# Attention-output units: last two operands made before the next unit's first, two operands to one ring tile

## Chip, cores, metric

One core of one Trainium2 chip. The metric is the device time of one execution in microseconds (us), lower being better. Three runs of the kernel before took 2354.53, 2354.87 and 2357.86 us, with a median of 2354.87 us.

## What is computed

One layer of a streaming encoder step, for 512 new frames of one stream and 64 frames of a second, cached one; the kernel carries all 576 frames side by side as columns. The reference, cut to what matters here:

```python
proj = rmsnorm(x, g_norm1) @ w_in            # 2048 -> 6144
o_attn = stick_breaking_blocks(q, k_all, v_all, P)   # 8 heads x 128
o_conv = gb * conv                            # 1024 channels
mix = concatenate([rmsnorm(o_attn, g_attn_out), rmsnorm(o_conv, g_conv_out)])
x = x + mix @ w_out                           # 2048 x 2048
x = x + (silu(h2 @ w_gate) * (h2 @ w_up)) @ w_down
```

The change sits in the product of the normed attention output with the upper half of `w_out` (rows 0 to 1023), which comes after the convolution's units and before the product with the lower half.

## The kernel before, in words

**Stages.** The heads' projections and the attention come first, then the convolution's columns of `w_in`, then the attention's half of `w_out`, then the convolution's half (`out_proj`, line 1256), then the feed-forward units. Every product is in fp32 made of two fp32r parts: a weight is split into a high part (a copy on ACT) and a low part (a subtraction on DVE), frames likewise, and three matmuls give one product.

**Attention-output units.** From line 993 on, the list `CU` holds nine convolution units and then eight output units, which this text calls U0 to U7 (in the code n = 9 to 16, kind `"o"`, `NCU` being 9). A unit is a block of 256 output columns against 1024 rows of `w_out`. It is done by a seven-product scheme for 2 by 2 blocks: p1 to p7, each with its own weight operand, made of the four blocks a11, a12, a21, a22 of the weights and sums of them. Here U3 p4 means product 4 of unit U3. One product of an output unit is 12 matmuls of 128 x 288 on 4 slices of 128 x 128 weights.

**Loads.** `call_columns` (line 1001) loads a unit's raw weights, 1 MB, with one DMA on SP's queue (line 1014) into one of the two places of `raw_a`. A place is called for again when the last operand that reads it (p3 and p4 of the unit that holds it) has been prepared (lines 1063 to 1067). So a unit's load goes out once p3 and p4 of the unit two before it are done.

**Making operands.** `conv_prepare` (line 1026) makes one operand. Before p6 it makes the sums own = a21 + a22 (line 1043), a21 -= a11 (line 1044) and a11 = own - a11 (line 1046), before p3 a12 -= a11 (line 1050), all on DVE and mostly in place. Then comes the high part on ACT (line 1055) and the low part on DVE (line 1058). The operand lies in a tile `whl` of a ring of four: two tags, `whi` and `wlo`, with two buffers each, taken in turn (line 1053). A tile has room for 8 slices, and an output unit's operand fills 4 of them. A tile comes free when the product that reads it has run.

**Running products.** `conv_run` (line 1090) issues a product's matmuls and the evacuations. p1, p6 and p5 accumulate in one PSUM bank (`psy`), followed by p3; after each of the first three ACT copies the bank to a tile `part` (line 1095), and the next product on that bank waits for the copy. p7 and p4 share another bank (`psw`). DVE adds bank and part into the result `x2` (line 1106) after p2, after p5 (this one reads the `psw` bank, and p4 waits for it) and after p4 (this one frees the part that the next unit's p6 writes). ACT copies the last block after p3 (line 1104).

**Order.** `corder` (line 1209) is the order in which products run. From U3 on it reads, for unit n: n p1, then p3 and p4 of unit n-1, then n p2, p6, p7, p5 (the last unit, U7, goes on with p6, p7, p5, p2, p4, p3). After the product at place k the operand at place k+4 is prepared (line 1233). The program writes out the order of PE by itself, and SP's in this stage as well; on ACT and DVE the scheduler sets the order by its own estimate of when things are ready, and in the trace each of these engines keeps to the order that was built: an instruction that waits there holds up those behind it.

**Neighbours on the DMA engines.** SP also issues `mixm`, the convolution's normed output (line 1179, 2304 KB right behind U4's load, and another part right behind U7's). POOL issues, after each unit, an accumulating read of the residual input into `x2` (line 1182, 576 KB). After the stage come the split weights of `out_proj` (lines 177 and 178), which use the same ring.

## Time and profile before

| | us |
|---|---|
| median of three runs | 2354.87 |
| the profiled execution's own time | 2357.63 |
| span of its profile | 2355.9 |
| PE busy in the span | 2335.7 |
| stage of the output units, from the first matmul of U0 to the last of U7 | 682 to 774 |
| time of one product of an output unit, from one start to the next | 1.59 |

The profile is of one execution; times within it are counted from the start of the span, and 1.7 us lie outside the span. A row of the timeline shows start, duration, engine, line, operation, the tiles (out<-in) with their shapes, how many instructions were merged, and in brackets the idle time before with what ended it. The granted TensorE clock is 1.00 in every stage that matters here.

### The profile page before, as it was taken

To read this page: it belongs to the slowest core of one execution; us is meant where nothing else is said; L and a number is where in the kernel's file an instruction comes from. 1 tells how busy PE (TensorE), PEld (TensorE's weight loads), DVE (VectorE), ACT (ScalarE), POOL (GpSimd) and SP (SyncE) were. 2 spreads that over 40 slices of the span, in tenths; PEclk is the share of its full clock that TensorE was granted. 3 is DMA by queue.
4 is the path that set the end of the run, shared out by engine and by line. 5 is a ranking of instruction groups with operands and counts; after the bars stand their busy time and mean duration, and the time that the engine had idled before them with its cause. 6 is when DMAs were issued, how large, how long until landed. Compare 5 with 4: busy or idle time off the path is not lost.

```text
span 2355.9 us, 43774 instructions
## 1 busy us (share of the span) xinstructions
PE 2335.7 (99%) x17573; PEld 2326.5 (99%) x17573; DVE 1890.2 (80%) x2822; ACT 1138.5 (48%) x1989; POOL 298.6 (13%) x401
## 2 busy tenths in 40 slices
PE   9999999999999999999999999999999999999999
PEld 8999999989999999999999999999999999999999
DVE  7766665788887899888888888888888778887896
ACT  6655565434444555444444444444444444444444
POOL 1111111422121230000000000000000002431221
PEclk9999999999999999999999999999999999999999
DMA  8665563773468555344344444444444936885553
GB/s 267 164 167 145 135 163 108 247 232 114 124 235 225 177 170 162 123 154 152 123 153 137 139 153 140 135 153 128 148 153 131 355 122 201 226 238 189 199 133 101
DMA packets 581795, 395.74 MB, mean 168 GB/s; under 512 B 90718, under 2 KB 570712, under 8 KB 581592
## 3 DMA queue, kind: packets, MB, share of 16 engines
q1 hardware_dynamic: 572168, 376.28, 51.2%
q0 software_dynamic: 8624, 16.22, 3.3%
q8 instruction: 137, 2.24, 0.4%
q14 instruction: 66, 0.54, 0.1%
q10 hardware_dynamic: 800, 0.46, 0.1%
HBM read 301.46 MB, written 91.44 MB: 167 GB/s over the span
## 4 chain that ended last, share of the span: by engine, by line
PE 86%; DVE 8%; DMA 3%; ACT 2%; issue 1%; POOL 0%; SPq 0%; DVEq 0%; ACTq 0%; POOLq 0%
PE psy L1582 34%; PE psw L1582 17%; PE pj L221 13%; PE psx L1582 9%; PE psy L1086 5%; PE psw L1086 3%; PE psx L1086 1%; DMA raw_a<-in_w_out_dram 1%; DVE wlo L178 1%; DMA raw_a<-in_w_in_dram 1%; DVE whl L231 1%; DVE whl L1058 1%; PE z L723 1%; PE pjo L221 1%; PE po L794 1%
## 5 line engine op out<-in xcount | busy, mean ns | idle before, releaser
L1582 PE MATMUL psy<-h_s,whl 128*128 128x288 f32 x2787 | 411.1, 294 | 0.0
L221 PE MATMUL pj<-x,whi 128*128 128x288 f32 x1856 | 388.6, 298 | 0.3 <-DVE x L375 0.3
L1582 PEld LDWEIGHTS psy<-h_s,whl 128*128 128x128 f32 x2787 | 383.2, 188 | 0.1
L231 DVE TENSOR_TENSOR whl<-raw_a,whl 128x1024 fp32r<-128x1024 f32 (+4 forms) x296 | 322.4, 1090 | 56.7 <-ACT whl L230 55.4
L1582 PE MATMUL psw<-t,whl 128*128 128x288 f32 x2400 | 347.2, 294 | 0.0
L1582 PEld LDWEIGHTS psw<-t,whl 128*128 128x128 f32 x2400 | 327.8, 188 | 0.0
L230 ACT CAST whl<-raw_a 128x1024 fp32r<-128x1024 f32 (+4 forms) x296 | 267.9, 906 | 113.3 <-issue 35.6
L221 PEld LDWEIGHTS pj<-x,whi 128*128 128x128 f32 x1856 | 303.9, 189 | 1.1 <-DVE x L375 0.7
L221 PE MATMUL pj<-x,wlo 128*128 128x288 f32 x928 | 274.5, 296 | 0.1
L231 DVE TENSOR_TENSOR whl<-raw_b,whl 128x1024 fp32r<-128x1024 f32 (+5 forms) x190 | 198.1, 1042 | 65.9 <-ACT whl L230 65.0
L230 ACT CAST whl<-raw_b 128x1024 fp32r<-128x1024 f32 (+5 forms) x190 | 165.0, 871 | 169.8 <-issue 72.8
L1592 ACT COPY part<-psy 128x288 f32<-128x288 f32 x242 | 96.5, 399 | 273.9 <-PE psy L1582 271.2
L1582 PE MATMUL psy<-b22m,whl 128*128 128x288 f32 x1212 | 182.7, 294 | 0.8 <-ACT part L1592 0.8
L1582 PE MATMUL psy<-t2t,whl 128*128 128x288 f32 x1212 | 183.0, 294 | 0.0
L221 PEld LDWEIGHTS pj<-x,wlo 128*128 128x128 f32 x928 | 174.8, 188 | 0.7 <-DVE wlo L442 0.3
L1582 PE MATMUL psx<-h_s,whl 128*128 128x288 f32 x1185 | 173.5, 294 | 0.0
L1582 PEld LDWEIGHTS psy<-b22m,whl 128*128 128x128 f32 x1212 | 168.0, 188 | 1.0 <-ACT part L1592 1.0
L1582 PEld LDWEIGHTS psy<-t2t,whl 128*128 128x128 f32 x1212 | 168.3, 188 | 0.2 <-DVE whl L231 0.2
L1582 PEld LDWEIGHTS psx<-h_s,whl 128*128 128x128 f32 x1185 | 162.6, 188 | 0.0
L1361 POOL DMA_DIRECT2D hid_dram<-form x3 | 2.2, 749 | 947.2 <-DVE form L231 947.2
L230 ACT CAST whl<-s 128x1024 fp32r<-128x1024 f32 (+5 forms) x81 | 72.2, 892 | 99.4 <-PE psw L1582 99.2
L1582 PE MATMUL psy<-t,whl 128*128 128x288 f32 x576 | 106.6, 295 | 0.0
(474 smaller groups left out, 4306.6 us busy)
## 6 DMA issues: line engine op xcount, KB each, us to landing
hid_dram<-form SPq DMA_DIRECT2D x147, 288.0 KB, 2.3
raw_a<-in_w_in_dram SPq DMA_DIRECT2D x41, 1024.0 KB, 6.0
raw_a<-in_w_gate_dram SPq DMA_DIRECT2D x22, 1024.0 KB, 5.5
raw_a<-in_w_up_dram SPq DMA_DIRECT2D x22, 1024.0 KB, 5.9
raw_b<-in_w_gate_dram SPq DMA_DIRECT2D x22, 1024.0 KB, 6.6
raw_b<-in_w_up_dram SPq DMA_DIRECT2D x22, 1024.0 KB, 6.9
h_s<-hid_dram SPq DMA_DIRECT2D x10, 2016.0 KB, 12.3
raw_a<-in_w_out_dram SPq DMA_DIRECT2D x16, 1024.0 KB, 5.7
```

The source lines that it names most:

```text
L178: lo_eng.tensor_tensor(out=lo[:, a:b], in0=raw[:, a:b], in1=hi[:, a:b].bitcast(F32), op=ALU.subtract)
L221: mm(ps, w_[:, k, csl], x_, start=(k == 0 and n == 0), stop=(k == nk - 1 and n == 2))
L230: nc.scalar.copy(out=hi, in_=src)
L231: (lo_eng or nc.vector).tensor_tensor(out=lo, in0=src, in1=hi.bitcast(F32), op=ALU.subtract)
L723: mm(zb[i], a_[:, kk], b_[:, q0:TP], start=(n == 0), stop=False, skip_group_check=True)
L794: mm(po[:, i * P : 512], a_[:, i, :], b_[:, : 512 - i * P], stop=(i == 0 and n == 2), **kw)
L1058: tt(out=whl[:, 1], in0=src, in1=whl[:, 0].bitcast(F32), op=ALU.subtract)
L1086: mm(ps, whl[:, w_, j, :], x_, start=(start and j == 0 and q == 0), stop=(j == m - 1 and q == 2), skip_group_check=True)
L1361: q.dma_start(out=hid_dram[fp][2 * n - 2 : 2 * n].rearrange("f p t -> p f t"), in_=t.bitcast(F32))
L1582: mm(ps, whl[:, w_, j, :], x_, start=(start and j == 0 and q == 0), stop=(j == len(xs_) - 1 and q == 2), skip_group_check=True)
L1592: nc.scalar.copy(out=t, in_=st["y"])
```

## The change

Two things are done, both for output units alone.

Two operands share a tile of the ring. The first operand takes a tile and leaves its second half in `bt["pair"]`; the next takes that half and no tile of its own. The ring of four tiles then holds eight operands, and a tile comes free once both of its products have run.

The order of preparing is no longer the order of running. From U3 on, in `porder`, p3 and p4 of unit n-1 are prepared ahead of n p1. The products run as before.

```diff
         src = at[p_]
         cturn[0] += 1
-        whl = wpool.tile([P, 2, NP, P], F32R, tag=("whi", "wlo")[cturn[0] % 2], name="whl")[:, :, :m]
+        if early or "pair" not in bt:
+            whl = wpool.tile([P, 2, NP, P], F32R, tag=("whi", "wlo")[cturn[0] % 2], name="whl")
+            if not early:
+                bt["pair"] = whl[:, :, m:]
+            whl = whl[:, :, :m]
+        else:
+            cturn[0] -= 1
+            whl = bt.pop("pair")
         coper[n, p_] = whl
...
+    porder = list(corder)
+    for k_, (n, p_) in enumerate(corder):
+        if p_ == 1 and n > NCU + 2:
+            porder[k_ : k_ + 3] = [*corder[k_ + 1 : k_ + 3], (n, p_)]
...
         for q in begin[k_] if k_ < len(begin) else range(k_ + 4, min(k_ + 5, len(corder))):
-            conv_prepare(*corder[q])
+            conv_prepare(*porder[q])
```

Built, the changed kernel has the same instructions in the same order on PE, SP and POOL. On ACT and DVE the order differs inside this stage alone.

## Prediction

> **What bounds the kernel now.** I read the page first: its span, the row of the engines and the chain's shares.

> ```profile
> span 2355.9 us, 43774 instructions
> PE 2335.7 (99%) x17573; PEld 2326.5 (99%) x17573; DVE 1890.2 (80%) x2822; ACT 1138.5 (48%) x1989; POOL 298.6 (13%) x401
> PE 86%; DVE 8%; DMA 3%; ACT 2%; issue 1%; POOL 0%; SPq 0%; DVEq 0%; ACTq 0%; POOLq 0%
> ```

> PE is busy all but 20 us of the span. The change keeps its matmuls and their order, so a gain can only come out of PE's idle time, and only inside the stage of the output units. The view of busy time by stretches, the waits of PE around this stage, and its timeline give that:

> ```profile
> 682.00:774.00 92.00, 90.74 (x684) 90.24 (x684) 68.70 (x120) 47.14 (x97) 12.12 (x12) 1.00 0.84 243
> PE psy L1086 <- ACT part L1095: 1.3, 2, 0.7
> 722.04 4.92 PE L1086 MATMUL psy<-forms,whl 128*128 128x288 f32 x36
> 726.80 1.75 PE L1086 MATMUL psw<-forms,whl 128*128 128x288 f32 x12
> 731.56 1.74 PE L1086 MATMUL psw<-forms,whl 128*128 128x288 f32 x12
> 733.86 5.03 PE L1086 MATMUL psy<-forms,whl 128*128 128x288 f32 x36 [0.56 <-ACT part L1095]
> 743.48 1.75 PE L1086 MATMUL psw<-forms,whl 128*128 128x288 f32 x12
> 745.94 5.06 PE L1086 MATMUL psy<-forms,whl 128*128 128x288 f32 x36 [0.70 <-ACT part L1095]
> ```

> Two stalls and no more. One product takes 1.587 us from start to start (722.04 to 726.80 is three). So U4 p5 was due at 731.56 + 1.59 = 733.15 and began at 733.86, 0.71 late; U5 p5 was due at 745.07 and began at 745.94, 0.87 late. Together 1.58 us; the idle column shows 1.26, because a matmul's modelled end runs over into the next one's start. The chain of work that ended last tells where they come from:

> ```profile
> 724.46 7.77 DMA raw_a<-in_w_out_dram
> 732.26 0.69 DVE cx L1043
> 732.95 0.38 DVE x L1106
> 733.41 0.41 ACT part L1095
> 733.86 1.87 PE psy L1086 x12
> ...
> 737.45 6.87 DMA raw_a<-in_w_out_dram
> 744.34 0.69 DVE cx L1043
> ```

> U5's weights are asked for at 724.46 and land 7.8 us later. DVE stands at the first sum of U5 (L1043); behind it is queued the add that frees the part of U3 p4, the copy of U4 p6 needs that part, and U4 p5 needs the copy. It is a load's landing, handed on by an engine that keeps its order. And it is a loop: landing 732.26, next issue 737.45, 5.19 us in which DVE makes U4's p3 and p4; then 6.87 us of load: 12.1 to 13.0 us a turn, where PE needs 7 x 1.587 = 11.1 us a unit.

> **The change part by part.**

> *Work.* No matmul, cast, subtraction, sum or DMA is added or removed: 56 operands, 8 loads. The price per instruction is unchanged: 0.

> *The ring.* Eight operands in place of four. Preparing waits for the product eight before, not four before; a tile is held until its second product has run, at most one or two products (3.2 us) longer, out of a lead that grows by four products (6.3 us). The split of `out_proj`'s first weight takes the ring's tiles after U7, and its tiles come free no later. No stall of PE is now put down to the ring, so by itself this buys 0.

> *The order: when U5's load goes out.* In the built order DVE does U3's p3 and p4 right behind the first two sums of U4 (L1043, L1044), with nothing else between. These rows price it:

> ```profile
> 712.51 0.37 SPq L1014 DMA_DIRECT2D raw_a<-in_w_out_dram  x1
> 713.18 0.72 SPq L1179 DMA_DIRECT2D mixm<-mix_dram  x1
> 706.17 1.75 PE L1086 MATMUL psx<-forms,whl 128*128 128x288 f32 x12
> 711.06 1.42 DVE L1058 TENSOR_TENSOR whl<-raw_a,whl 128x512 fp32r<-128x512 f32 x2
> 715.89 0.40 ACT L1104 COPY x<-psy 128x288 f32<-128x288 f32 x1 [0.67 <-PE psy L1086]
> 733.70 1.14 ACT L1055 CAST whl<-raw_a 128x512 fp32r<-128x512 f32 x2
> 723.15 1.29 DVE L1058 TENSOR_TENSOR whl<-raw_a,whl 128x512 fp32r<-128x512 f32 x2
> 732.87 0.45 DVE L1106 TENSOR_TENSOR x<-psw,part 128x288 f32<-128x288 f32 x1
> 712.51 6.75 DMA raw_a<-in_w_out_dram
> ```

> Before, U4's load followed U2's p3 and p4 (711.06) and went out at 712.51. Now those two stand ahead of the add after U2 p2, whose matmuls end at 707.92, so U4's load goes out at about 708.0 (estimate), 4.5 us sooner. With its 6.75 us it lands at 714.8. The two sums take 2 x 0.60 (half the pitch of two DVE instructions, 1.29 less 0.09 of overlap), to 716.0. ACT's casts of U3 p3 and p4 stand behind its copy at 715.89 (done by 716.3) and take 1.14, to 717.4; the second subtraction ends 0.7 later, and U5's load leaves at 718.1: 6.3 us sooner than 724.46.

> *The order: when U5's load is needed.* This is what the diff does not show. The scheduler has moved U5's first sums forward as well: L1043 and L1044 of U5 now stand ahead of the add after U3 p5, which U3 p4 waits for, and U3 p4 begins at 726.80. Before, the landing was needed for U4 p5 at 733.15. From landing to product it is now 0.60 + 0.60 + 0.45 + 0.15 of hand-over = 1.8 us (1.6 before, 732.26 to 733.86). So the load must land by 725.0, and 725.0 - 718.1 = 6.9 us are allowed, where 731.55 - 724.46 = 7.1 were. Issue and need have moved together. For U6's and U7's loads the same distance holds, 6.9 us.

> *How long the load takes.* Bounds from the nearest rows:

> ```profile
> DMA to landing us min/median/max: 5.5/5.7/7.8
> mixm<-mix_dram SPq DMA_DIRECT2D x1, 2304.0 KB, 13.5
> 720.97 1.20 POOL L1182 DMA_DIRECT2D x<-xt_dram  x1 [9.47 <-DVE whl L1058]
> ```

> 5.5 us alone, 13.5 for the big `mixm` transfer. `mixm` goes out 0.67 us behind U4's load, so now at 708.7, and lands at 722.2; U5's load leaves with 722.2 - 718.1 = 4.1 us of it left, before with 713.18 + 13.5 - 724.46 = 2.2. If the load waits for all that is left, it takes 7.8 + 1.9 = 9.7 us; if for nothing more, 7.8. POOL's residual read (720.97) ran into it before and will again. I take the middle, 8.8, and keep 5.5 to 13.5 for the range. U3 p4 is then 8.8 - 6.9 = 1.9 us late. U6's load has no `mixm` beside it: 6.87 as before, 0 to 0.1 late. U7's load is allowed 6.9 too and took 5.9 before (749.52 to 755.38): 0.

> ```profile
> 749.52 0.37 SPq L1014 DMA_DIRECT2D raw_a<-in_w_out_dram  x1
> 755.38 0.69 DVE L1043 TENSOR_TENSOR cx<-raw_a 128x512 f32<-128x512 f32 x1 [2.70 <-DMA raw_a<-in_w_out_dram]
> ```

> [...]

> *Elsewhere.* U2's and U3's loads follow p3 and p4 of U0 and U1, which are made no later than before:

> ```profile
> 696.64 0.40 SPq L1014 DMA_DIRECT2D raw_a<-in_w_out_dram  x1
> 700.11 0.40 SPq L1014 DMA_DIRECT2D raw_a<-in_w_out_dram  x1
> 705.75 0.69 DVE L1043 TENSOR_TENSOR cx<-raw_a 128x512 f32<-128x512 f32 x1
> 707.76 1.75 PE L1086 MATMUL psy<-forms,whl 128*128 128x288 f32 x12
> ```

> The earliest that anything waits for U3's is the cast of U3 p1 on ACT, now ahead of the copy that U2 p6 (707.76) needs: landed by 706.7 costs 0, and it was there by 705.75 already. `out_proj`'s first split ends ahead of PE as before, and from there on PE has the same work and the same waits.

> *Sum,* against the profiled execution: -1.58 (both stalls go) + 1.9 (U3 p4) + 0.1 (U4 p4, for U6's load) = +0.4 us: span 2356.3, and with the 1.7 us outside it 2358.0, where that execution took 2357.6. It stands 2.8 us above the median of the runs; from the median 2354.87 the forecast is **2355.3 us**.

> **The rivals.**

> *The cover holds.* U5's load needs 6.9 us or less, because the DMA engines give it a fair share beside `mixm`. For it: of the four loads in the rows above three took 5.9 to 6.9. Against it: 7.8 in the same company. Price: both stalls gone, -1.58, 2353.3 us. No larger gain is to be had here.

> *The load queues up (slower).* SP's transfers are served one after another, the residual reads of U3 and U4 fall into the same stretch, and U5's load takes what another 1 MB class transfer took in a full stretch:

> ```profile
> forms<-form_dram SPq DMA_DIRECT2D x7, 1152.0 KB, 13.2
> ```

> At 13.5 us U3 p4 is 6.6 late: +6.6 + 0.1 - 1.58 = +5.1, 2360.0 us. If U4's, U6's and U7's loads did so too, a turn of the loop would be 13.2 + 2.6 = 15.8 us against PE's 11.1, near 20 us in all. It turns slower than before at 8.4 us (6.9 + 1.5), and passes 0.2% at 13.1. Against it: those transfers stood seven deep, here two.

> [...]

> *It does nothing.* If SP holds U5's load back for something other than U3's p3 and p4, it leaves and lands as before, with the two stalls in other places: 2354.9 us. The row of the issue, 0.02 us behind the last subtraction (723.15 + 1.29), speaks against it.

> **How the numbers follow.** The forecast (load of U5 at 7.3 to 11 us, 2353.8 to 2357.5) has 0.53; the cover holds 0.30; nothing happens 0.06; the load queues up 0.09, of which 0.08 passes 0.2%; something outside the stage that gains over 0.2%, 0.02. The range runs from 2352.8 (the cover holds, and 0.5 of scatter) to 2358.5 (the forecast's upper end and 1.0 of scatter; the runs before scatter by 3.3). 0.2% is 4.7 us, about what a measurement of this kernel can tell from no change. Faster by over that 0.02, within it 0.90, slower 0.08.

> **What would show it.** The issue of U5's load near 718 and U4's near 708 on SP's timeline; PE's idle time before U4 p5 and U5 p5 gone; a wait of a `psw` product at about 726.8 (U3 p4) on the add of L1106, as long as U5's landing is past 725.0; U5's load at 8 to 10 us; all else equal. It would be wrong if that `psw` product does not wait, if the load takes under 7 us, if PE waits on casts of U3's or U4's p1, which are now made last of their three, or if the stage grows by more than 3 us.

## The result and the profile after

The changed kernel took 2361.51 us (median of nine runs, 2359.95 to 2367.77); the kernel before, beside it, 2357.62 us (nine runs, 2354.53 to 2359.06). The ratio is 1.0024, 95% interval 1.0016 to 1.0032: slower by 3.9 us. Run again later (`after_again`) it took 2361.57 us beside 2356.52 us, 1.0023 (1.0014 to 1.0031). The forecast was 2355.3 us in a range of 2352.8 to 2358.5, so it is wrong.

The profiled execution took 2367.77 us, the longest of the nine, with a span of 2366.1 us, 10.2 us more than before. In the changed kernel lines from 1061 on stand 7 lower and those from 1236 on 11 lower: L1086 is now L1093, L1106 is L1113. Its page, and then the stretch that was shown of before:

```profile
span 2366.1 us, 43748 instructions
PE 2340.8 (99%) x17573; PEld 2331.7 (99%) x17573; DVE 1888.2 (80%) x2822; ACT 1137.4 (48%) x1989; POOL 302.1 (13%) x401
```

```profile
682.00:774.00 92.00, 87.78 (x645) 87.52 (x645) 65.13 (x114) 44.74 (x92) 11.52 (x11) 0.96 0.81 235
```

Each engine in that row has as many instructions as before. In the same 92 us PE is busy 3 us less, does 39 matmuls fewer (645 for 684), and its clock is 0.96. PE's timeline has all of it:

```profile
721.36 4.92 PE L1093 MATMUL psy<-forms,whl 128*128 128x288 f32 x36
730.49 3.25 PE L1093 MATMUL psw<-forms,whl 128*128 128x288 f32 x12 [4.22 <-DVE x L1113]
733.54 2.82 PE L1093 MATMUL psx<-forms,whl 128*128 128x288 f32 x12
736.19 1.78 PE L1093 MATMUL psy<-forms,whl 128*128 128x288 f32 x12
772.99 1.75 PE L1093 MATMUL psx<-forms,whl 128*128 128x288 f32 x12
775.27 0.67 PE L1093 MATMUL psw<-forms,whl 128*128 128x288 f32 x3 [0.53 <-DVE x L1113]
```

The two old waits, before U4 p5 and U5 p5, are gone (-1.58 us). U3 p4 was due at 721.36 + 3 x 1.587 = 726.12 and began at 730.49, **4.37 us late**. From there U3 p4 took 3.05 us to the next start and U4 p2 2.65, where a product takes 1.587: **2.53 us more**. At the end U7 p4 (775.27) was 0.69 late. The sum is +6.0, and that is what the stage grew by, from 91.32 us (682.23 to 773.55, where the next stage's first matmul starts) to 97.30 (681.55 to 778.85). The chain that ended last says why U3 p4 waited:

```profile
716.16 1.30 DVE whl L1065 x2
...
717.49 11.15 DMA raw_a<-in_w_out_dram
...
728.65 0.70 DVE cx L1043
...
729.99 0.46 DVE x L1113
...
730.49 3.25 PE psw L1093 x12
```

U5's load goes out at 717.49, behind U3's p3 and p4, and lands 11.15 us later. DVE makes U5's two first sums, then the add (729.99), then PE goes on: 1.85 us from landing to product. Why the two products behind the wait are slow is in the view of stretches, whose column ahead of the DMA share is the granted clock:

```profile
726.00:728.00 2.00, 0.28 (x3) 0.04 (x1) 0.00 (x0) 0.40 (x1) 0.00 (x0) 1.00 0.26 52
728.00:730.00 2.00, 0.00 (x0) 0.00 (x0) 1.31 (x3) 0.00 (x0) 0.00 (x0) 0.77 0.01 4
730.00:732.00 2.00, 1.51 (x6) 1.51 (x7) 1.64 (x4) 0.00 (x0) 0.00 (x0) 0.50 0.00 0
734.00:736.00 2.00, 2.00 (x10) 2.00 (x10) 1.53 (x3) 0.97 (x2) 1.13 (x1) 0.53 0.00 0
736.00:738.00 2.00, 2.00 (x17) 2.00 (x16) 1.35 (x3) 0.62 (x1) 0.07 (x1) 1.00 0.74 141
```

While PE was idle the clock fell to half (0.50 from 729.07), and it came back only at 735.9; PE did 10 matmuls in 2 us there, not 17.

Of the 10.2 us, 6.0 are this stage. The stage began 0.7 us sooner, and from its end to the end of the span went 1587.25 us where before had 1582.35. This last part belongs for the most part to this one execution: in the second trace of the same kernel it was 1583.35 (`after_again`, below).

The theory with which I began the experiments: U5's load is long because it now shares the DMA engines with more of `mixm`; DVE's built order hands its landing on to U3 p4; and the idle time costs again through the clock. The rivals: the ring or the order does the harm by itself, POOL's residual read makes the load long, or the clock falls for another reason.

### The profile page after: what moved, and what is told of

It is laid out like the page before. It is cut to its first block, busy times and chain, and to the rows that moved or that the text cites. A ratio compares the mean times of both kernels' runs of the same rounds, so it can differ in the third digit from the quotient of the medians.

```text
span 2366.1 us, 43748 instructions
## 1 busy us (share of the span) xinstructions
PE 2340.8 (99%) x17573; PEld 2331.7 (99%) x17573; DVE 1888.2 (80%) x2822; ACT 1137.4 (48%) x1989; POOL 302.1 (13%) x401
## 4 chain that ended last, share of the span: by engine, by line
PE 87%; DVE 7%; DMA 2%; ACT 2%; issue 1%; POOL 0%; SPq 0%; DVEq 0%; ACTq 0%; POOLq 0%
PE psy L1593 34%; PE psw L1593 17%; PE pj L221 13%; PE psx L1593 9%; PE psy L1093 6%; PE psw L1093 3%; PE psx L1093 1%; DVE wlo L178 1%; DMA raw_a<-in_w_in_dram 1%; PE z L723 1%; PE pjo L221 1%; PE po L794 1%; DMA raw_a<-in_w_out_dram 0%; DVE po L1280 0%; DVE whl L1065 0%
## 5 line engine op out<-in xcount | busy, mean ns | idle before, releaser
L230 ACT CAST whl<-s 128x1024 fp32r<-128x1024 f32 (+5 forms) x81 | 72.3, 892 | 99.8 <-PE psw L1593 97.3
```

The lines of the kernel that those rows point to most:

```text
L230: nc.scalar.copy(out=hi, in_=src)
```

## The experiments

All kernels are compared with the kernel before on the same chip. "Late" is the start of a product less the start that 0.132 us a matmul gives.

**One part alone.** The pairing without the new order, and the new order without the pairing:

```diff
-            conv_prepare(*porder[q])
+            conv_prepare(*corder[q])
```

> Two operands to a tile, operands made in the order of before. Theory A (late load): it is the ring's eight operands that let the scheduler put U5's first sums ahead of the add that U3 p4 waits for, so the need for U5's load is still near 725.0; but U3's p3 and p4 are made behind U4's p1 again, so the load goes out near 721.0, 3 us later than with both parts. A load of 8.5 to 10 us then makes U3 p4 4.5 to 6 us late, U2 p6 and U4 p4 some 0.7 each, and after so long an idle time the granted clock falls to 0.50 again for +2.5 us: stage 97 to 100 us, time 6 to 9 us above the kernel before. Rival B (the order does the harm, the ring is neutral): stage 91 to 92 us, time within 1 us of the kernel before, no wait of U3 p4.

It took 2364.01 us beside 2356.91 (1.0028, 1.0017 to 1.0039); the stage was 98.26 us.

```profile
718.28 11.20 DMA raw_a<-in_w_out_dram
```

```profile
730.62 3.25 PE L1093 MATMUL psw<-forms,whl 128*128 128x288 f32 x12 [4.29 <-DVE x L1113]
```

The first row is from its chain, the second from PE's timeline. The pairing alone brings the same wait, 4.44 us late, and the same clock (1.46 + 0.90 us). So it is the ring of eight that lets the scheduler put U5's sums ahead of the add, and B falls: the ring is not neutral. The load went out at 718.3, though, not at 721.0, and U2 p6 and U4 p4 were on time (U7 p4 was 1.38 late): the ring alone makes the load earlier too, which theory A had put down to the order.

```diff
-        if early or "pair" not in bt:
...
+        whl = wpool.tile([P, 2, NP, P], F32R, tag=("whi", "wlo")[cturn[0] % 2], name="whl")[:, :, :m]
```

> Operands made in the new order, one to a tile as before. Theory A: with four operands in the ring the scheduler cannot move U5's sums so far forward; U5's load goes out near 723.4 and is first needed for U4 p7, 6.5 us later. At 7.8 us U4 p7 is 1.3 late, with 0.6 and 0.4 at the same product of U3 and U5: stage about 91.5 to 92.5 us, PE never idle for 2 us at a time, granted clock 1.00, time 0 to +2 us beside the kernel before. Rival B (the order itself does the harm): a wait of 4 us or more as in the changed kernel, the clock at 0.50 behind it, time +4 us.

2360.57 us beside 2356.91 (1.0020, 1.0010 to 1.0030), stage 97.79 us: theory A's figures missed, and rival B's wait of 4 us did not come either. PE's timeline, and the clock of a stretch:

```profile
721.59 2.22 PE L1086 MATMUL psw<-forms,whl 128*128 128x288 f32 x11 [2.25 <-DVE whl L1058]
723.60 6.03 PE L1086 MATMUL psy<-forms,whl 128*128 128x288 f32 x36
748.15 1.76 PE L1086 MATMUL psw<-forms,whl 128*128 128x288 f32 x11 [2.49 <-DVE whl L1058]
```

```profile
722.50:726.00 3.50, 3.50 (x18) 3.50 (x17) 1.98 (x3) 0.62 (x1) 0.26 (x1) 0.51 1.10 259
```

U3 p7 and U5 p7 wait 2.4 and 2.7 us, because here U4's and U6's loads took 8.72 and 8.99 us, and DVE waits for them at L1043, ahead of the low parts of these operands; U6 p7 waits 0.9 in the same way. The order by itself is therefore no gain either, though by another wait. Unexpected is the clock: behind an idle time of 2.25 us it went to 0.50 here (1.7 us more for the products behind it), while 2.49 us at U5 p7 left it at 1.00.

**Who stands behind the load on DVE.** DVE and ACT held to the written order, in which U5's sums stand behind U3's and U4's adds:

```diff
+        if (n, p_) == (NCU + 2, 1):
+            turn_mode.enter_context(tc.manual_schedule(engines={mybir.EngineType.Activation, mybir.EngineType.DVE}))
```

> The changed kernel with DVE and ACT held to the order in which the program is written, from U2 p1 to the end of the stage. Theory A: U5's two sums then stand behind the adds of U3 and U4; the load goes out near 722.8 and is needed only for U5 p1, 10 us later, so no product waits for it even at 11 us; left is about 1 us before U7 p4. Stage about 90.7 us, granted clock 1.00, time 0 to 1.5 us under the kernel before. Rival C (the transfer is what counts, whoever stands behind it): a wait of 3 to 4 us on U5's load remains and the time stays 4 us above the kernel before.

2356.45 us beside 2356.91 (1.0000, 0.9991 to 1.0009), stage 91.99 us. No product of U2 to U6 waits; left are two in U7:

```profile
764.37 1.85 PE L1093 MATMUL psy<-forms,whl 128*128 128x288 f32 x12 [0.88 <-ACT part L1102]
768.88 0.67 PE L1093 MATMUL psw<-forms,whl 128*128 128x288 f32 x3 [1.08 <-DVE x L1113]
```

These are U7 p5 and U7 p4 (1.04 and 1.24 late; I had counted one of them). In the written order U7 p5's copy stands on ACT behind the norm factor of the convolution's half (lines 492 and 493), U7 p4's add on DVE behind U7 p3's low part and another step of that norm (line 231). The harm of the change is undone by order alone. The run changes two things, though: U5's load also goes out later, at 721.08, and took 7.5 us. Its first reader, ACT's cast of U5 p1, comes near 731.3, so a load of 11.15 us would have been some 0.9 us late (estimate). Rival C's 3 to 4 us fall; how much of the cure is the shorter load, this run does not tell. Ended at U7 p6, the written order leaves 0.5 us there:

> The changed kernel with DVE and ACT in written order from U2 p1 only up to U7 p6; the two late products of U7 in the run with written order to the end (0.88 and 1.08 us) stood behind work for the next stage. Theory A: U5's load goes out near 721 to 723 and nothing waits for it; what is left is 0.6 us before U7 p4. Stage 90.3 to 91 us (91.3 in the kernel before, 97.3 with the change), granted clock 1.00, time 0.5 to 1.5 us under the kernel before, less than a comparison of times can settle. Rival C: a wait of 3 us or more on U5's load in the last units.

2355.87 us beside 2356.52 (0.9995, 0.9987 to 1.0004), stage 90.30 us, as theory A had it. The kernel before with the written order to the end of the stage:

> The kernel before with DVE and ACT in written order to the end of the stage, as in the run with written order of the changed kernel (stage 92.0 us). Theory A (what counts is who stands behind the load on DVE, not the ring and the order): U5's load goes out near 724 and is needed only for U5 p1; no wait on it; two late products of U7, about 1 us each, as there. Stage 91 to 92 us, time within 1 us of the kernel before. Rival B3 (only the ring of eight and the new order give the lead): a wait of 1 us or more in the middle of the stage, stage over 93 us.

2358.36 us beside 2356.53 (1.0008, 0.9999 to 1.0017), stage 92.93 us, with 1.14 and 1.28 late in U7 and one wait left in the middle: U4 p5, 0.40 late, because here ACT's cast of U5 p1 waits for U5's load ahead of the copy. Neither theory's figures are met: the written order takes nearly all of the middle's waits away without ring and order, but the stage stays 0.9 us above that of `manual`.

**The clock.** Thirty matmuls ahead of U3 p4, whose result nobody reads:

```diff
+            if n == NCU + 3:
+                idle = misc("idle")[:, :HALF]
+                for q in range(FILL):
+                    mm(idle, oner, ft[1][:, 0, 0, :], start=(q == 0), stop=(q == FILL - 1))
```

> The changed kernel with 30 matmuls of 128x288 (0.132 us each, 4.0 us) ahead of U3 p4, whose result nobody reads: PE works while U3 p4 waits. Theory A: the wait of U3 p4 stays (it begins near 730.5), but the granted clock stays at 1.00 behind it, U3 p4 and U4 p2 take 1.6 us each, and the stage is 2.5 us shorter than with the change alone: about 94.8 us; time about 2.5 us under the changed kernel. Rival D (the clock fell for another reason than the idle time): 0.50 again from 730 to 736 and a stage of 97 us.

```profile
724.76 4.16 PE L1161 MATMUL idle<-forms,oner 128*128 128x288 f32 x30
728.80 1.86 PE L1094 MATMUL psw<-forms,whl 128*128 128x288 f32 x12
730.50 1.75 PE L1094 MATMUL psx<-forms,whl 128*128 128x288 f32 x12
```

U3 p4 is nearly as late as in the changed kernel (due 724.76, begun 728.80: 4.04 us), but the two products behind it take 1.70 and 1.58 us, the clock is 1.00 throughout, and the stage is 94.40 us, 2.9 under that of the change. So the fall came with the idle time, and without it stayed away; rival D falls. The time does not follow: 2362.85 us beside 2356.91 (1.0026, 1.0016 to 1.0036), no less than the changed kernel. Its profiled execution was the shortest of its eight (2360.24). The mean granted clock of all eight was 0.999 to 1.000, as in the kernel before, so it was not the clock that the others spent more on; what it was stays open.

**What makes the load long.** `mixm`'s first transfer in two, the second half behind U5's load:

```diff
-        for i in range(2):
-            yield 80
...
+        for i, wait, parts_ in ((0, 80, ((0, 0, 4),)), (0, 28, ((0, 4, NG),)), (1, 52, ((1, 0, NG - 1), (2, NG - 1, NG)))):
+            yield wait
```

> The changed kernel with the first transfer of mixm (2304 KB) in two of 1152 KB: one behind U4's load as before, the other only behind U5's load. Theory A1 (U5's load is long because mixm's bytes are still ahead of it): half of mixm is through before U5's load goes out near 717.5, so that load has only POOL's residual read for company and takes 7.5 to 9 us; U3 p4 is 0.5 to 2 us late, granted clock 1.00, stage 91 to 93 us (97.3 with the change alone), time within 1 us of the kernel before. Rival A2 (POOL's residual read, which leaves 1 us behind U5's load, is what makes it long): still 10.5 us or more, U3 p4 over 3.5 us late, the clock at 0.50, stage 96 to 98 us.

2355.69 us beside 2356.52 (0.9997, 0.9988 to 1.0006), stage 90.26 us, the clock at 1.00. SP's and DVE's timelines:

```profile
718.96 0.37 SPq L1014 DMA_DIRECT2D raw_a<-in_w_out_dram  x1
724.22 0.69 DVE L1043 TENSOR_TENSOR cx<-raw_a 128x512 f32<-128x512 f32 x1 [0.48 <-DMA raw_a<-in_w_out_dram]
```

U5's load took 5.2 us, less than I expected of A1. The residual read was still issued 1.4 us behind it, but this does not settle A2. What the DMA engines moved from the load's issue to its landing (q1 is SP's queue, q0 POOL's; packets, MB, then the share of 16 engines' time):

```profile
q1 hardware_dynamic: 1283, 1.31, 78.8%
q0 software_dynamic: 9, 0.01, 1.2%
```

Only 0.01 MB of the read's 0.59 had moved when the load landed; the rest came behind it. So this run took both neighbours away from the load and cannot tell A1 from A2. The residual reads put later in the program:

```diff
-            add_x(n - NCU)
+            if n == NCU + 6:
+                for d in range(6):
+                    add_x(d)
+            if n >= NCU + 6:
+                add_x(n - NCU)
```

> The changed kernel with POOL's residual reads of U0 to U5 all put behind U6, so that none runs beside U5's load. In the changed kernel's trace, from U5's issue to its landing, the software queue had 27.3% of 16 engines' time over 11.1 us; without it the same bytes of SP's queue need about 3 us less. Theory A1 (mixm is the main part, the residual read some): load 8 to 9 us, U3 p4 1 to 2 us late, clock 1.00, stage 92 to 93 us. Rival A2 (the residual read is nearly all of it): load under 7.3 us, U3 p4 on time. If neither matters: 11 us again. Six reads in a row then run beside U7's and out_proj's loads, which may cost up to 3 us further on, so the time says less than the stage.

2362.09 us beside 2356.52 (1.0027, 1.0016 to 1.0037), but the edit did not do what it says:

```profile
718.47 1.20 POOL L1189 DMA_DIRECT2D x<-xt_dram  x1 [8.98 <-DVE whl L1065]
```

POOL's order is built too, and U2's read left 1 us behind U5's load as ever. It is one more trace of the change: load 10.7 us, U3 p4 3.90 late, stage 96.08 us. With POOL's order written out, and U2's read behind U6's:

```diff
-            add_x(n - NCU)
+            if n != NCU + 2:
+                add_x(n - NCU)
+            if n == NCU + 6:
+                add_x(2)
```

> The changed kernel with POOL's order written out and the residual read of U2 (near 718.5, 1 us behind U5's load) put behind that of U6, so that U5's load has only mixm for company; in resid_later POOL had kept its old order, so this is that question again. Theory A1 (what is left of mixm when the load goes out, plus 5.3 to 5.7 us as in mix_split and before_split): 4.1 us of mixm left and 5.5 of its own, 9.2 to 9.8 us, where the four traces with the read beside it had 10.0 to 11.2; U3 p4 2.3 to 3.1 us late, the clock perhaps at 0.50 for 3.4 us; stage 92 to 95.5 us. Rival A2 (the residual read is the main part): 7 us or less, U3 p4 on time, stage under 91 us. If the read does nothing: 10 to 11.2 us again.

2356.85 us beside 2356.77 (1.0001, 0.9992 to 1.0011), stage 91.75 us, the mean granted clock of the profiled execution 1.000. SP's, DVE's and PE's timelines:

```profile
715.90 23.98 SPq L1014 DMA_DIRECT2D raw_a<-in_w_out_dram  x3
723.97 0.69 DVE L1043 TENSOR_TENSOR cx<-raw_a 128x512 f32<-128x512 f32 x1 [3.29 <-DMA raw_a<-in_w_out_dram]
725.81 1.88 PE L1093 MATMUL psw<-forms,whl 128*128 128x288 f32 x12 [1.11 <-DVE x L1113]
```

8.05 us and 1.27 late: under A1's 9.2, over A2's 7. Both transfers counted here: with what is left of `mixm` for company the load takes 8.05 us where `mix_split` had 5.2, and with the read as well 10.0 to 11.2. What the DMA engines moved from U5's issue to its landing, in before, in the changed kernel, and in this one:

```profile
DMA packets 1429, 1.75 MB, mean 226 GB/s; under 512 B 47, under 2 KB 1174, under 8 KB 1429
q1 hardware_dynamic: 1158, 1.17, 42.6%
q0 software_dynamic: 271, 0.59, 40.8%
```

```profile
DMA packets 2453, 2.95 MB, mean 264 GB/s; under 512 B 49, under 2 KB 2196, under 8 KB 2452
q1 hardware_dynamic: 2179, 2.34, 60.2%
q0 software_dynamic: 273, 0.59, 28.2%
```

```profile
DMA packets 2128, 2.30 MB, mean 286 GB/s; under 512 B 42, under 2 KB 2114, under 8 KB 2127
q1 hardware_dynamic: 2104, 2.26, 78.9%
q0 software_dynamic: 23, 0.03, 2.0%
```

The load itself is 1.05 MB. In before 0.12 MB of SP's other bytes went through ahead of the landing; in the changed kernel 1.29 MB did. The residual read's 0.59 MB is beside it in both, and it is dear for its size: in the changed kernel 28.2% of the engines' time for a fifth of the bytes. In these traces more bytes took longer (`mix_split` 1.34 MB in 5.2 us, then 1.75 in 7.8, 2.30 in 8.05, 2.95 in 11.15), but bytes alone do not give the time, as the next run shows.

The split in the kernel before:

> The kernel before, with mixm's first transfer in two as in mix_split. Theory A1 (a load is long by what is ahead of it on the DMA engines): U5's load, issued near 724.5, takes 5 to 6 us in place of 7.8, so U4 p5 begins on time; U6's load may meet the second half and stay at 6.5 to 7 us, so up to 0.9 us is left before U5 p5. Stage 89.9 to 90.8 us (91.3 before), time 0.5 to 1.5 us under the kernel before. Rival B2 (the split helps only together with the new order): both old waits stay, stage 91.3 us.

2355.11 us beside 2356.53 (0.9992, 0.9983 to 1.0001), the lowest median of these runs, but the interval reaches past 1, so the times alone do not show a gain. U5's load took 5.65 us (issued 723.97). The first two rows say what was moved in it, the others are from PE's timeline:

```profile
DMA packets 1471, 1.73 MB, mean 308 GB/s; under 512 B 32, under 2 KB 1291, under 8 KB 1471
q0 software_dynamic: 196, 0.41, 40.7%
732.70 4.92 PE L1086 MATMUL psy<-forms,whl 128*128 128x288 f32 x36
743.80 4.92 PE L1086 MATMUL psy<-forms,whl 128*128 128x288 f32 x36
```

The last two are the rows of U4 p5 and U5 p5, late by 0.71 and 0.87 in before and on time here; one product earlier on, U2 p6, takes 0.3 us longer. The stage is 89.75 us, 1.57 less: as much as the change was to gain. B2 falls. But as many bytes (1.73 MB) went through in 5.65 us as took 7.8 in before. There the last 2 us moved 84 GB/s and less; here the engines moved some 390 up to the landing, with the second half of `mixm` behind the load. What makes that thin end, and why it is gone, no run shows. Both cures in the changed kernel:

> The changed kernel with both cures: written order up to U7 p6 and mixm's first transfer in two. Theory A: each cure alone takes the wait away (stages of 90.3 us both), so together they give nothing more: 90.2 to 90.6 us, with about 0.4 us left before U7 p4; time 0.5 to 1.5 us under the kernel before. If the two added up, the stage would be under 89.9.

2355.61 us beside 2356.53 (0.9994, 0.9985 to 1.0003), stage 90.28 us, as expected: they do not add up.

**The change once more.**

> The changed kernel once more, for a second trace. Theory A: the stage is 96 to 98.5 us again, with U3 p4 4 to 5 us late and the granted clock at 0.50 behind it; the wait of 2.8 us ahead of the feed-forward part, with the clock down to 0.64 behind it, belongs to that one execution, and is 1.4 to 1.8 us with the clock at 1.00 this time; stage end to end of the span 1582 to 1584 us; time 4 to 6 us above the kernel before. Rival E (that wait comes from the change): 2.8 us again, 1586 to 1588 us.

Stage 95.54 us, U3 p4 3.24 us late (load 10.0 us), and 2359.9 - 776.55 = 1583.35 us from the stage's end to the end of the span:

```profile
728.82 2.02 PE L1093 MATMUL psw<-forms,whl 128*128 128x288 f32 x12 [3.08 <-DVE x L1113]
```

```profile
730.50:733.50 3.00, 3.00 (x14) 3.00 (x13) 1.75 (x3) 1.14 (x2) 1.20 (x1) 0.50 0.02 8
```

```profile
PE ss L500 <- ACT sq L230: 2.4, 1, 2.4
```

Stage and lateness are a little under A's lower bounds, and the clock is at 0.50 again. The rest of the span is in A's range. The wait ahead of the feed-forward part, the last row, is not: 2.4 us, with 2.8 and 2.5 in the other two traces of the change (the first, and `resid_later`), and 1.3 to 1.7 in every other kernel. In these three traces the transfer of the first feed-forward weights, issued at the same distance from the stage's end as in before (95.4 us), moves slowly in its middle: under 200 GB/s for 2.1 to 2.6 us, and 70, 5 and 83 GB/s at the slowest, where before kept to 233 and more. It does so in `order_only` too (73 GB/s), whose wait was 1.5. The clock from 850 to 1000, the stretch that holds this wait, was 0.99, where before had 1.00 and A expected 1.00. So E keeps a part of about 1 us, and its cause stays open.

| kernel | stage | U5's load | late for it | median - before |
|---|---|---|---|---|
| before | 91.32 | 7.8 | 0.71 (U4 p5) | 0 |
| changed | 97.30 | 11.15 | 4.37 (U3 p4) | +3.9 |
| changed, again | 95.54 | 10.0 | 3.24 (U3 p4) | +5.0 |
| mix_split | 90.26 | 5.2 | 0 | -0.8 |
| resid_u2 | 91.75 | 8.05 | 1.27 (U3 p4) | +0.1 |
| before_split | 89.75 | 5.65 | 0 | -1.4 |

## Why the prediction was wrong, step by step

*The base:* the forecast was counted from 2354.87, the median of three runs. Nine runs of the same kernel gave 2357.62, so 2.75 of the 6.2 us between forecast and result are the base and not the change. The range moved up by as much would end at 2361.25, still below the result.

*Work, and the two old waits:* right; the same 17573 matmuls, and -1.58 us.

*The ring, "by itself this buys 0":* wrong. It let the scheduler move U5's sums ahead of the add; alone it cost 6.9 us of stage (98.26 for 91.32). The prediction saw the moved sums in the built order, but put them down to the order of preparing.

*When U5's load goes out and when it is needed:* right. U4's at 706.61 (about 708.0 predicted), U5's at 717.49 (718.1), 1.85 us from landing to product (1.8), and U3 p4 waiting on the add as long as the landing was late.

*How long the load takes:* **the first step that failed.** It took the middle, 8.8 us, and 11.15, 10.7 and 10.0 were measured: 1.2 to 2.35 us more. The reason given, 4.1 us of `mixm` left in place of 2.2, came from `mixm`'s time to landing, and that time was right (4.2 us: 707.28 + 14.4 - 717.49). In bytes the difference was 1.29 MB for 0.12. The landings here can have a thin end (in the last 2 us before the landing of U5's load 40 GB/s and less were moved, where some 390 went at the start), so the remaining time says little about what is still to be moved. The bound of 13.5 us held.

*The price of a late product:* **the second step.** It counted U3 p4's lateness and nothing behind it. At half clock the products behind cost 1.6 to 2.5 us more. The second trace shows that this step fails by itself: its load of 10.0 us lies inside the forecast's 7.3 to 11, its lateness of 3.24 us is what the forecast's rule gives (10.0 - 6.9 = 3.1), and still the stage grew by 4.2 us where that rule has +1.6. The trace of before had a hint of it, at the start of its timeline of PE, where PE had been idle for 4.9 us:

```profile
10.08 0.68 PE L221 MATMUL pj<-x,whi 128*128 128x288 f32 x2
10.56 0.44 PE L221 MATMUL pj<-x,wlo 128*128 128x288 f32 x1
...
12.65 0.43 PE L221 MATMUL pj<-x,whi 128*128 128x288 f32 x2
12.92 0.30 PE L221 MATMUL pj<-x,wlo 128*128 128x288 f32 x1
```

Two of these matmuls take 0.48 us from start to start, and 2.6 us later 0.27, although the clock column says 1.00 there.

*Elsewhere, "the same waits":* wrong by 0.7 to 1.0 us at U7 p4, whose add stands behind `out_proj`'s split on DVE, and by the open part ahead of the feed-forward units.

So +0.4 became -1.58 + 4.37 + 2.53 + 0.69 = +6.0 in the profiled execution and -1.58 + 3.24 + 1.67 + 1.01 = +4.3 in the second (4.2 measured); the medians say +3.9 and +5.0. The loop's range for U6's and U7's loads held: no wait there.

*The rivals.* "The load queues up" gave 2360.0 us, nearest of all, from the right stretch and a wait too long (6.6 us) that stood in for the clock's share; some of that nearness is luck, as the low base took 2.75 us off. Its chance of 0.09 was too low: the load's range went to 13.5 us, and the two companions in the quoted rows both pointed upwards. "The cover holds" fell, and so did "it does nothing".

The case in which the load waits for all that is left of `mixm`, an estimate from the rows of before, gave 9.7 us. The traces lie above it with the residual read beside the load (10.0 to 11.15) and below it without (8.05), so it named the right direction against this change, and not the size; the order in which the transfers are served was not shown.

## What to carry to other kernels

Where a change issues a transfer earlier, count the bytes that will be ahead of it and beside it on the DMA engines, other queues included (here 1.29 MB of SP's other bytes and 0.59 MB of the residual read, for a load of 1.05); its old duration, and the time that its neighbour has left, said little here (8.8 us expected from them, 11.15 measured). The bytes gave the direction here, not the time to a microsecond (1.73 MB in 5.65 us, 1.75 in 7.8). The wait on this load cost half as much again behind it (2.53 us behind 4.37, 1.67 behind 3.24), so price such a wait with its clock, and not by its length alone: an idle time of 2.25 us had 0.50 behind it, one of 2.49 us 1.00. Where a ring gets deeper, look at the built order of the engine that receives the load: room to look ahead moved its waiting instruction in front of work that was safe (`ring_only`, 4.44 us late).

## What was not expected of the hardware

The granted clock fell to 0.50 and stayed there for 6.8 or 3.4 us. In half-microsecond stretches it was low from 729.1 to 735.9 in the changed kernel and from 728.8 to 735.6 in `ring_only` (6.8 us each), and for 3.4 us in `after_again` (730.34 to 733.75), `resid_later` (729.82 to 733.26) and `order_only` (722.55 to 725.95). In these five it fell 2.5 to 4.6 us after PE's idle time had begun (726.33 in `ring_only`, 725.74 in `after_again`); in `after_again` and `order_only` PE was at work again by then.

The length of the wait did not decide it. Gaps of 2.25 us (`order_only`, U3 p7) and 3.08 us (`after_again`, U3 p4) brought the fall, one of 2.49 us (`order_only`, U5 p7) did not. From 850 to 1000 the clock was 0.99 in `mix_split`, whose wait ahead of the feed-forward part was 1.3 us, and 1.00 in before, whose wait there was 1.70. The rows are of `mix_split`: the wait, and the stretch that holds it:

```profile
PE ss L500 <- ACT sq L230: 1.3, 1, 1.3
850.00:1000.00 150.00, 148.51 (x1110) 148.07 (x1109) 133.52 (x196) 76.07 (x126) 11.38 (x11) 0.99 0.48 153
```

In the other traces the same shares can be estimated from the half-microsecond stretches and the timelines, with the periods laid out from the fall. Ahead of it PE was busy for about 0.27 of a period in `ring_only`, 0.45 in `after_again`, 0.34 in `order_only` and not at all in `resid_later`. The gap of 2.49 us in `order_only` was split between two periods, and in the emptier one (746.44 to 749.86) PE was busy for about 0.50: no fall. A first low period in which PE was busy for 0.47 (`ring_only`), 0.58 or 0.86 (the changed kernel) was followed by a second one, one with 0.94 (`resid_later`) or 1.00 (`after_again`, `order_only`) was not. The shares are what these traces show; no run set out to test where the limit lies.
